# A transformer encoder in one kernel: every gate behind the next pair's second sum, four shared buffers for the weight sums, and the memory's squares in the first chunk

## The chip, the cores and the metric

The kernel runs on one core of a Trainium2 chip. The metric is the device time of one execution in microseconds; the time before is the median of three runs, 2031.19 us (2030.74 to 2033.74). TensorE (PE in the profile) does the matmuls, VectorE is DVE, ScalarE is ACT, GpSimd is POOL, SyncE is SP.

## What is computed

Two encoder layers on 512 tokens of width 1024. Each layer has a half-step feed-forward block, a mixer with several kinds of attention, an attention over 256 memory tokens, and a second half-step feed-forward block. The change lies in the feed-forward blocks, which compute, on normalised tokens:

```python
D_MODEL = 1024
SEQ = 512
DEPTH = 2
N_MEM = 256
D_FF = 2816

def swiglu(x, wg, wu, wd):
    return (jax.nn.silu(x @ wg) * (x @ wu)) @ wd
```

The memory tokens are normalised too (`rmsnorm`), once, and the sums of squares for that are computed inside the first feed-forward block.

## The kernel before

**Stages.** The program has seven stretches in the profile: feed-forward 1 of layer 0 (0 to 343 us), mixer and memory attention (to 718), feed-forward 2 (to 1038), feed-forward 1 of layer 1 (to 1367), its mixer and memory attention (to 1690), and the last feed-forward (to 2030). They are called the first to fourth stage below where only the four feed-forward blocks are meant.

**A split product.** Each float32 operand is split in two, a high part rounded to TensorE's format (`wh`, `sh`, `t1h`, `hh`; ScalarE, a copy) and the rest (`wl`, `sl`, `t1l`, `hl`; VectorE, a subtraction). A product is high times high, high times low and low times high. For weights `operand` (L529) does this, for each of the seven products of a pair; its results go in turn to two shared buffers `wh`/`wl` or, every third time, to the stage's own pair `sh`/`sl` (`f.n % 3 == 2`).

**Pairs.** The 22 blocks of the hidden width go in pairs. Pair 0 is a plain product (`plain_pair`). Pairs 1 to 10 each compute gate and up projections for 256 hidden columns with a Strassen-like scheme of seven products instead of eight. Each product is 24 matmuls of 128x256, in `product` (L565), a product every 2.72 us. By the name of their token operand they come in this order: `t1` (`sum_pair`: the weights' sum s1), `t2` (the same sum less w11, the "second sum", L607), `21` (`cross_pair`: w12), `t3` (the third sum s3), then the next pair's `11` (`open_pair`: w11), then `t4` (w22) and `22` (`close_pair`: w12 less the second sum). `t1` to `t4` are token combinations, split once per stage by `token_sums` (L480 to L485). The weight sum s1 and the third sum s3 are made by a fetch on SP (L550) and an accumulating DMA of a second quarter on POOL (L601 and L633); s3 is negated on ScalarE between them (L632). Buffers: three for s1, one for s3, three (`wf`) for plain weights.

**Results.** The products accumulate in PSUM and are collected in `gu` by copies on ScalarE (L588, L614, L627, L638, L651) and additions on VectorE (L639, L659). The *crossed copy* is L638, after `t3`. Then comes the *gate*: gs = gu times R (L688, R is the normalising factor per token), silu (L690), times up (L691); `hidden_done` makes sums and differences for the paired down-projection (L700) and splits the result (`hh` on ScalarE L450, `hl` on VectorE L454, `th`, `xh` likewise, L710 and L715). Before the change the gate of pairs 1, 2, 3 and 7 is written behind the low part of the next pair's second sum (`f.lowered`); all other gates are written at once.

**Down-projection.** The hidden width is taken in chunks of 6, 8 and 8 blocks. The first two are done by `paired_down` with the same seven-product scheme, after pairs 3 and 7; the last by `down` at the end, with an early block (`down_products`, L835) between the `t3` product and the last two products of pair 10, whose weights are split into `sh`/`sl` (`block` with `own`, L169).

**Heads.** While pair 0 still runs, the sum of squares of the tokens gives `factor` (L405), then four transposes (L418) and a copy (L419) give R. Pair 0's own gate is L422, L430 and L432. After pair 2's `cross_pair`, `set_aside` writes the eight token blocks (256 KB each) to DRAM (L802; in the first stage the input itself is used and nothing is written), to make room for the down-projection's sums.

**Memory's squares.** In the first stage `mem_stats` fetches four of the eight memory blocks at a time, squares them on ScalarE (L259) at pairs 3 and 4 and adds them on POOL (L260); at pair 6 it makes the factor.

**Order.** TensorE's order is the order in which the code is written. That of the other engines and of the DMA issues comes from a scheduler that simulates a timeline; `high_priority` and `behind` (issue after a given instruction) steer it. On each engine the instructions then run in that order, and a DMA queue works in order too.

## Time and profile before

| | |
|---|---|
| median of three runs | 2031.19 us (2030.74 to 2033.74) |
| profiled execution | 2032.02 us, span 2030.2 us, granted clock 0.998 |
| TensorE | 2008.5 us, 99% of the span |
| VectorE | 1597.6 us, 79% |
| ScalarE | 1278.1 us, 63% |
| POOL | 357.0 us, 18% |
| chain that ended last | TensorE 93% |

In a timeline a row has the start in us, the length, the engine, the line, the operation, the tiles written and read (without buffer numbers), their shapes, the count of merged instructions, and in brackets the idle time before them and what ended it. Rows of windows have, for each engine asked for, busy time and count, then the clock granted to TensorE (1 is full), the DMA engines' share and GB/s. Rows of DMAs have the tile, the issuing engine's queue, the count, the size of one and the us from issue to landing.

### The profile page before, as it was taken

To read this page: it belongs to the slowest core of one execution; us is meant where nothing else is said; L and a number is where in the kernel's file an instruction comes from. 1 tells how busy PE (TensorE), PEld (TensorE's weight loads), DVE (VectorE), ACT (ScalarE), POOL (GpSimd) and SP (SyncE) were. 2 spreads that over 40 slices of the span, in tenths; PEclk is the share of its full clock that TensorE was granted. 3 is DMA by queue.
4 is the path that set the end of the run, shared out by engine and by line. 5 is a ranking of instruction groups with operands and counts; after the bars stand their busy time and mean duration, and the time that the engine had idled before them with its cause. 6 is when DMAs were issued, how large, how long until landed. Compare 5 with 4: busy or idle time off the path is not lost.

```text
span 2030.2 us, 35251 instructions
## 1 busy us (share of the span) xinstructions
PE 2008.5 (99%) x13849; PEld 1843.1 (91%) x13853; DVE 1597.6 (79%) x2363; ACT 1278.1 (63%) x1955; POOL 357.0 (18%) x339
## 2 busy tenths in 40 slices
PE   9999999999999999999999999999999999999999
PEld 7999998888888899999989999988888888999997
DVE  8979776699676798888679797864668788979784
ACT  7667564656786576665657665745768566766572
POOL 1021001356531111100010101003353111010100
PEclk9999999999999999999999999999999999999999
DMA  7777755322241277776467777544224324777763
GB/s 233 199 200 190 192 164 167 99 79 84 95 139 61 65 235 187 209 189 183 144 177 206 207 187 188 176 140 140 94 84 125 104 73 141 221 209 193 183 177 98
DMA packets 102263, 316.53 MB, mean 156 GB/s; under 512 B 11472, under 2 KB 14672, under 8 KB 102096
## 3 DMA queue, kind: packets, MB, share of 16 engines
q1 hardware_dynamic: 85680, 257.12, 38.6%
q0 software_dynamic: 16128, 56.63, 16.1%
q8 instruction: 109, 1.79, 0.3%
q14 instruction: 58, 0.48, 0.1%
q10 hardware_dynamic: 288, 0.52, 0.1%
HBM read 301.64 MB, written 12.58 MB: 155 GB/s over the span
## 4 chain that ended last, share of the span: by engine, by line
PE 93%; DVE 2%; ACT 2%; DMA 2%; issue 1%; POOL 0%; SPq 0%; DVEq 0%; ACTq 0%; POOLq 0%
PE ps_pa L565 35%; PE ps_pb L565 13%; PE ps_pa L958 13%; PE ps_pa L904 5%; PE ps_pa L835 4%; PE ps_pb L835 4%; PE ps_pb L1071 3%; PE ps_pa L399 2%; PE ps_pa L1561 2%; PE ps_pa L1392 2%; PE ps_pb L1124 1%; PE ps_pb L904 1%; PE ps_pb L1097 1%; PE ps_pa L1291 1%; PE ps_pb L399 1%; DMA s<-l_ffn_wq 1%
## 5 line engine op out<-in xcount | busy, mean ns | idle before, releaser
L169 ACT ACTIVATE wh<-wf 128x1024 fp32r<-128x1024 f32 (+1 forms) x155 | 154.4, 1002 | 178.7 <-issue 37.8
L541 ACT ACTIVATE wh<-s 128x1024 fp32r<-128x1024 f32 (+1 forms) x164 | 168.8, 1029 | 134.6 <-PE ps_pa L565 30.0
L542 DVE TENSOR_TENSOR wl<-s,wh 128x1024 fp32r<-128x1024 f32 (+1 forms) x164 | 193.6, 1182 | 57.9 <-ACT wh L541 55.7
L171 DVE TENSOR_TENSOR wl<-wf,wh 128x1024 fp32r<-128x1024 f32 (+1 forms) x110 | 128.9, 1177 | 43.1 <-ACT wh L169 39.8
L541 ACT ACTIVATE wh<-wf 128x1024 fp32r<-128x1024 f32 (+1 forms) x100 | 103.3, 1033 | 65.4 <-PE ps_pa L565 46.3
L171 POOL TENSOR_TENSOR wl<-wf,wh 128x1024 fp32r<-128x1024 f32 (+1 forms) x45 | 100.0, 2221 | 205.3 <-ACT wh L169 143.1
L542 DVE TENSOR_TENSOR wl<-wf,wh 128x1024 fp32r<-128x1024 f32 (+1 forms) x100 | 118.3, 1186 | 9.9 <-ACT wh L541 9.8
L633 POOL DMA_DIRECT2D s<-l_ffn_wq x40 | 35.1, 879 | 510.3 <-ACT s L632 234.7
L958 PE MATMUL ps_pa<-wh,xh 128*128 128x512 f32 x384 | 121.7, 398 | 0.0
L958 PE MATMUL ps_pa<-wh,xl 128*128 128x512 f32 x384 | 118.8, 391 | 0.0
L958 PE MATMUL ps_pa<-wl,xh 128*128 128x512 f32 x384 | 118.7, 390 | 0.0
L542 DVE TENSOR_TENSOR sl<-wf,sh 128x1024 fp32r<-128x1024 f32 (+1 forms) x68 | 80.3, 1180 | 19.8 <-ACT sh L541 19.8
L541 ACT ACTIVATE sh<-wf 128x1024 fp32r<-128x1024 f32 (+1 forms) x68 | 69.3, 1020 | 34.8 <-PE ps_pa L565 19.3
L958 PEld LDWEIGHTS ps_pa<-wh,xl 128*128 128x128 f32 x384 | 72.1, 188 | 15.7
L958 PEld LDWEIGHTS ps_pa<-wl,xh 128*128 128x128 f32 x384 | 72.0, 188 | 15.6
L542 DVE TENSOR_TENSOR sl<-s,sh 128x1024 fp32r<-128x1024 f32 (+1 forms) x60 | 71.1, 1185 | 17.9 <-ACT sh L541 17.8
L541 ACT ACTIVATE sh<-s 128x1024 fp32r<-128x1024 f32 (+1 forms) x60 | 62.0, 1033 | 36.7 <-PE ps_pb L565 12.9
L1086 ACT ACTIVATE e<-e,m 128x128 f32<-128x128 f32 (+3 forms) x128 | 70.7, 554 | 21.7 <-DVE m L1085 21.5
L958 PEld LDWEIGHTS ps_pa<-wh,xh 128*128 128x128 f32 x384 | 69.2, 188 | 12.3
L601 POOL DMA_DIRECT2D s<-l_ffn_wq x40 | 37.0, 932 | 236.6 <-DMA s<-l_ffn_wq 106.5
L565 PE MATMUL ps_pa<-xh,wh 128*128 128x256 f32 x472 | 73.6, 277 | 0.0
L565 PE MATMUL ps_pa<-xl,wh 128*128 128x256 f32 x472 | 73.1, 276 | 0.0
(460 smaller groups left out, 6204.1 us busy)
## 6 DMA issues: line engine op xcount, KB each, us to landing
wf<-l_ffn_wq SPq DMA_DIRECT2D x120, 512.0 KB, 4.5
s<-l_ffn_wq SPq DMA_DIRECT2D x80, 512.0 KB, 4.4
s<-l_ffn_wq POOLq DMA_DIRECT2D x80, 512.0 KB, 7.9
wf<-l_w_in SPq DMA_DIRECT2D x48, 512.0 KB, 3.4
wf<-l_ffn_wd SPq DMA_DIRECT2D x32, 512.0 KB, 3.7
wf<-l_ffn_wdq SPq DMA_DIRECT2D x24, 512.0 KB, 4.8
wf<-l_ffn_wdq SPq DMA_DIRECT2D x24, 384.0 KB, 3.7
s<-l_ffn_wdq SPq DMA_DIRECT2D x16, 512.0 KB, 3.8
```

The costliest lines, as they stand in the source:

```text
L169: self.leading = nc.scalar.activation(wh[:, sl], w[:, sl], AF.Copy)
L171: eng.tensor_sub(wl[:, sl], w[:, sl], wh.bitcast(F32)[:, sl])
L399: nc.tensor.matmul(p, w[a][:, k * P:(k + 1) * P], xs[k][c], start=k == order[0] and a == c == 0, stop=k == order[-1] and a == 1)
L541: self.leading = nc.scalar.activation(h, t, AF.Copy)
L542: self.parted = nc.vector.tensor_sub(l, t, h.bitcast(F32))
L565: self.nc.tensor.matmul(bank[:, z * 256:z * 256 + 256], w[a][:, o:o + P], xs[k][b], start=first and n == 0, stop=n == len(ops) - 1, skip_g ...
L835: self.nc.tensor.matmul(bank, w[a][:, j * P:(j + 1) * P], h, start=j == a == e == 0 and c < len(CHUNKS) - 1, stop=j == nb - 1 and (a, e) = ...
L904: nc.tensor.matmul(banks[dd], w[g, k // 2][a][:, o:o + P], parts(k)[b], start=k == first and a == b == 0, stop=k == last and a == 1)
L958: nc.tensor.matmul(banks[j], xs[k][a][:, j * P:(j + 1) * P], w[b][:, kk * 512:kk * 512 + 512], start=k == a == b == 0, stop=k == KB - 1 an ...
L1071: nc.tensor.matmul(bank[:, o:o + n], a, b[:, :n], start=c == 0, stop=c == len(ops) - 1)
L1086: nc.scalar.activation(e, e, AF.Exp, bias=m[:, i:i + 1], scale=-1.0, accum_out=rs[:, i:i + 1])
L1392: nc.tensor.matmul(banks[c][i], a[:, i * P:(i + 1) * P], b[:, c * 512:(c + 1) * 512], start=(k == 0 and n == 0), stop=(k == KB - 1 and n = ...
```

## The change

Six edits, in the four feed-forward stages:

1. Every gate but the last pair's is written behind the low part of the next pair's second sum, and the rounding of its result (`hh`, and the rest of `hidden_parts` with it) behind the crossed copy of that next pair.
2. s1 and s3 share one set of four buffers instead of three and one, in `paired_down` too.
3. The early block of the last chunk is written as two runs: four blocks through all three kinds of product, then two.
4. The rotation of the operand buffers begins at 2, so the first operand of pair 1 (w11) gets the stage's own tiles, and all later ones move by two places.
5. The copies after `t2` and `t3` (L614 and L638 before) get high priority, and the low part of pair 1's s1 is put behind `factor`.
6. The memory blocks are fetched all at once at pair 2; the squares come in one run ahead of the first paired down-projection, their additions on VectorE instead of POOL.

What this does to the order: VectorE at the opening of pair 1 in the second stage, before. `s1` is the weight sum (L542 its high part's remainder, L607 the second sum), t2l to t4l the token combinations, gs pair 0's gate, `wf` w12.

```order
L542 TENSOR_TENSOR wl_8117<-s1_8113,wh_8116 128x1024
L405 COPY factor_8006<-r_8004 128x4
L607 TENSOR_TENSOR s1_8113<-s1_8113,wf_8055 128x1024
L483 TENSOR_TENSOR t2l_8151<-tq_8032,t2h_8149 128x1024
L419 COPY R_8088<-ps_pb_8087 128x512
L542 TENSOR_TENSOR sl_8156<-s1_8113,sh_8154 128x1024
L542 TENSOR_TENSOR wl_8188<-wf_8185,wh_8187 128x1024
L422 TENSOR_TENSOR gs_8094<-ps_pa_7907,R_8088 128x512
L422 TENSOR_TENSOR gs_8094<-ps_pa_7969,R_8088 128x512
L483 TENSOR_TENSOR t3l_8227<-tq_8033,t3h_8225 128x1024
```

The same place on VectorE after the change:

```order
L407 COPY factor_8005<-r_8003 128x4
L546 TENSOR_TENSOR wl_8119<-s1_8115,wh_8118 128x1024
L421 COPY R_8090<-ps_pb_8089 128x512
L611 TENSOR_TENSOR s1_8115<-s1_8115,wf_8054 128x1024
L486 TENSOR_TENSOR t2l_8153<-tq_8031,t2h_8151 128x1024
L424 TENSOR_TENSOR gs_8096<-ps_pa_7906,R_8090 128x512
L424 TENSOR_TENSOR gs_8096<-ps_pa_7968,R_8090 128x512
L486 TENSOR_TENSOR t3l_8226<-tq_8032,t3h_8224 128x1024
L546 TENSOR_TENSOR wl_8156<-s1_8115,wh_8155 128x1024
L546 TENSOR_TENSOR sl_8187<-wf_8184,sh_8186 128x1024
```

The second sum's low part (sl_8156 before, wl_8156 after) has moved behind pair 0's two multiplications by R and behind t3l, and the factor ahead of the first sum's low part. The first and the fourth stage show the same; in the third the second sum's low part stays ahead of these three.

SP's DMA issues in the same place, before: s1 and s3 are weight sums of pairs 1 to 3, wf_8055 is w11 and wf_8185 w12 of pair 1, wf_8256 w11 of pair 2, kept the set-aside writes.

```order
L550 DMA s1_8113<-l0_ffn2_wq 128x1024
L550 DMA wf_8055<-l0_ffn2_wq 128x1024
L550 DMA s3_8217<-l0_ffn2_wq 128x1024
L550 DMA s1_8355<-l0_ffn2_wq 128x1024
L550 DMA s1_8612<-l0_ffn2_wq 128x1024
L550 DMA wf_8185<-l0_ffn2_wq 128x1024
L550 DMA wf_8256<-l0_ffn2_wq 128x1024
L550 DMA wf_8289<-l0_ffn2_wq 128x1024
L550 DMA s3_8469<-l0_ffn2_wq 128x1024
L802 DMA kept_8503<-x_6744 128x512 x2
```

And after; wf_8184 is now w12 of pair 1:

```order
L554 DMA s1_8115<-l0_ffn2_wq 128x1024
L554 DMA wf_8054<-l0_ffn2_wq 128x1024
L554 DMA s3_8216<-l0_ffn2_wq 128x1024
L554 DMA s1_8354<-l0_ffn2_wq 128x1024
L554 DMA s3_8454<-l0_ffn2_wq 128x1024
L808 DMA kept_8502<-x_6743 128x512 x2
L808 DMA kept_8502<-x_6750 128x512 x2
L808 DMA kept_8502<-x_7138 128x512
L554 DMA wf_8184<-l0_ffn2_wq 128x1024
L808 DMA kept_8502<-x_7138 128x512
```

The third sum of pair 2 has moved up to the fifth place, and five of the eight writes, which are tied to it, stand ahead of w12. The fourth stage shows the same; in the third all eight stand ahead of w12.

VectorE at pair 5 of the second stage, before and then after: s1 is pair 5's sum, the first row its second sum (before L607, after L611), gs the gate of pair 4.

```order
L607 TENSOR_TENSOR s1_9471<-s1_9471,wf_9357 128x1024
L659 TENSOR_TENSOR gu_8788<-gu_8788,ps_pb_9210 128x2x256
L542 TENSOR_TENSOR wl_9535<-wf_9532,wh_9534 128x1024
L688 TENSOR_TENSOR gs_9451<-gu_8788,R_8088 128x1024
L542 TENSOR_TENSOR sl_9504<-s1_9471,sh_9503 128x1024
```

```order
L611 TENSOR_TENSOR s1_9451<-s1_9451,wf_9356 128x1024
L665 TENSOR_TENSOR gu_8787<-gu_8787,ps_pb_9209 128x2x256
L546 TENSOR_TENSOR sl_9520<-wf_9517,sh_9519 128x1024
L546 TENSOR_TENSOR wl_9484<-s1_9451,wh_9483 128x1024
L694 TENSOR_TENSOR gs_9512<-gu_8787,R_8090 128x1024
```

The gate's multiplication has gone from ahead of the second sum's low part to behind it.

The diff, without the lines that only pass an argument on:

```diff
-            f = self.f = SimpleNamespace(pre=pre, ctx=ctx, hp=pool("h"), tp=pool("t"), H={}, n=0, taken=None, own=False, low=None, gate=None, ahead=None, spread=None, macc=None,
+            f = self.f = SimpleNamespace(pre=pre, ctx=ctx, hp=pool("h"), tp=pool("t"), H={}, n=2, taken=None, own=False, low=None, gate=None, ahead=None, spread=None, macc=None,
...
+                hide = None
                 if f.gate is not None:
                     f.gate, gate = None, f.gate
-                    gate(f.lowered)
+                    hide = gate(f.lowered)
...
                 self.cross_pair(pair)
+                if hide is not None:
+                    hide()
...
-                    self.down_products(c, early, LEAD + REST, False)
+                    self.down_products(c, early, LEAD + REST, False, range(CHUNKS[c] - 4))
+                    self.down_products(c, early, LEAD + REST, False, range(CHUNKS[c] - 4, CHUNKS[c] - 2))
...
-                    gate = self.close_pair(old, False)
-                    if p <= 2 or p in ends:
-                        f.gate = gate
-                    else:
-                        gate()
+                    f.gate = self.close_pair(old, False)
                     if c in PAIRED and p == ends[c]:
+                        if self.mem_r is None and c == 0:
+                            self.mem_squares()
                         self.paired_down(c)
...
-        nc.scalar.activation(hh[:, sl], h, AF.Copy)
+        with self.behind(after):
+            nc.scalar.activation(hh[:, sl], h, AF.Copy)
...
-        self.parted = nc.vector.tensor_sub(l, t, h.bitcast(F32))
+        with self.behind(after):
+            self.parted = nc.vector.tensor_sub(l, t, h.bitcast(F32))
...
-            pair.s = f.tp.tile([P, 1024], F32, name="s1", tag="s1", bufs=3)
+            pair.s = f.tp.tile([P, 1024], F32, name="s1", tag="s1", bufs=4)
...
-            w = self.operand(pair.s)
+            w = self.operand(pair.s, None, f.factored if p == 1 else None)
...
-        nc.scalar.copy(self.corner(pair, 0, 1), self.halves(pair.y))
+        with self.tc.high_priority():
+            nc.scalar.copy(self.corner(pair, 0, 1), self.halves(pair.y))
...
-            s = f.tp.tile([P, 1024], F32, name="s3", tag="s3", bufs=1)
+            s = f.tp.tile([P, 1024], F32, name="s3", tag="s1", bufs=4)
...
-        f.taken = nc.scalar.copy(c, self.halves(pair.y))
+        with self.tc.high_priority():
+            f.taken = nc.scalar.copy(c, self.halves(pair.y))
...
-            self.hidden_done(p, gs, t)
+            return lambda: self.hidden_done(p, gs, t, False, f.taken)
...
+    def mem_squares(self):
+
+        with self.behind(self.leading):
+            for m in self.f.mem:
+                self.f.macc = self.square(self.f.macc, m, NMEM, self.nc.vector)
```

More of the change, by code (lines that the diff above doesn't have):

```diff
@@ L433, in hidden, with hidden_done @@
         self.hidden_done(p, gs, t, True)
-    def hidden_done(self, p, h, t, later=False):
+    def hidden_done(self, p, h, t, later=False, after=None):
         for c in PAIRED:
@@ L439, in hidden_done, with hidden_parts @@
             if 0 <= j < CHUNKS[c] // 2:
-                return self.hidden_sums(p, j, h, t, later)
-        self.hidden_parts(p, h, 0, later)
-    def hidden_parts(self, p, h, b0, later=False):
+                return self.hidden_sums(p, j, h, t, later, after)
+        self.hidden_parts(p, h, 0, later, after)
+    def hidden_parts(self, p, h, b0, later=False, after=None):
         nc, f = self.nc, self.f
@@ L527, in own_tiles, with operand @@
         return tiles
-    def operand(self, t, own=None):
+    def operand(self, t, own=None, after=None):
         nc, f = self.nc, self.f
@@ L691, in gates, with hidden_sums @@
             nc.vector.tensor_mul(two(gs), two(t), gu[:, :, 1, :])
-            self.hidden_done(p, gs, t)
+            return lambda: self.hidden_done(p, gs, t, False, f.taken)
         return gates
-    def hidden_sums(self, p, j, h, t, later):
+    def hidden_sums(self, p, j, h, t, later, after):
         nc, f = self.nc, self.f
@@ L704, in hidden_sums @@
         sub(part(t, 2), part(h, 2), part(t, 1))
-        self.hidden_parts(p, h, 0, later)
+        self.hidden_parts(p, h, 0, later, after)
         two = [f.hp.tile([P, S], F32R, name=n, tag="T", bufs=max(CHUNKS)) for n in ("th", "tl")]
@@ L1439, in mem_keys @@
         return kh, kl, vp
+    def mem_squares(self):
+        with self.behind(self.leading):
+            for m in self.f.mem:
+                self.f.macc = self.square(self.f.macc, m, NMEM, self.nc.vector)
     def mem_stats(self, p):
         nc, f = self.nc, self.f
-        if p in MEM_SQUARES:
-            with self.behind(self.leading):
-                for m in f.mem:
-                    f.macc = self.square(f.macc, m, NMEM)
-        if p + 1 in MEM_SQUARES:
-            n = KB // len(MEM_SQUARES)
-            f.mem, loaded = [], self.loaded
-            for k in range(MEM_SQUARES.index(p + 1) * n, MEM_SQUARES.index(p + 1) * n + n):
-                if k % 2 == 0:
-                    two = f.hp.tile([P, S], F32, name="mem", tag="T", bufs=max(CHUNKS))
-                m = two[:, k % 2 * NMEM:k % 2 * NMEM + NMEM]
+        if p == MEM_FETCH:
+            rooms = [f.hp.tile([P, 1024], F32, name="mem", tag="H", bufs=max(CHUNKS))]
+            rooms += [f.hp.tile([P, S], F32, name="mem", tag="T", bufs=max(CHUNKS)) for _ in range(2)]
+            f.mem = [t[:, o:o + NMEM] for t in rooms for o in range(0, t.shape[-1], NMEM)]
+            loaded = self.loaded
+            for k, m in enumerate(f.mem):
                 with self.behind(loaded):
                     nc.sync.dma_start(m, self.I["memT"][k * P:(k + 1) * P, :])
-                f.mem.append(m)
         if p == MEM_FACTOR:
```

6 lines of the change are left out of this document (3 added, 3 removed).

## The prediction

> **What bounds the kernel now.** I read the page first (busy times, chain), then TensorE's waits, then the timelines of the engines around each of these waits. From the page, the busy times and the chain of work that ended last, by engine:
>
> ```profile
> PE 2008.5 (99%) x13849; PEld 1843.1 (91%) x13853; DVE 1597.6 (79%) x2363; ACT 1278.1 (63%) x1955; POOL 357.0 (18%) x339
> PE 93%; DVE 2%; ACT 2%; DMA 2%; issue 1%; POOL 0%; SPq 0%; DVEq 0%; ACTq 0%; POOLq 0%
> ```
>
> TensorE is the bound, and the change gives it the same products. So the time moves only by what TensorE waits, and by the clock it is granted. The waits of TensorE in the four feed-forward stages (engine, bank and line, what it waited for: us in all, times, longest):
>
> ```profile
> PE ps_pa L565 <- DVE wl L542: 3.0, 5, 0.7
> PE ps_pa L835 <- ACT sh L169: 2.8, 4, 0.7
> PE ps_pa L565 <- DVE sl L542: 2.6, 4, 0.7
> PE ps_pa L565 <- ACT gu L614: 2.6, 1, 2.6
> PE ps_pa L565 <- ACT gu L638: 1.1, 1, 1.1
> PE ps_pa L565 <- ACT wh L541: 0.7, 1, 0.7
> PE ps_pb L418 <- DVE factor L405: 0.4, 1, 0.4
> ```
>
> These 13.2 us are all that the change can win directly; whatever it adds can be much more, since a late operand stops TensorE outright.
>
> **Pair 4 of the first stage.** Timelines of POOL, ACT and TensorE, two stretches of TensorE (busy time, matmul records, granted clock), and one of all engines in the paired down-projection before (PE, PEld, DVE, ACT, POOL busy):
>
> ```profile
> 120.45 1.18 POOL L633 DMA_DIRECT2D s<-l_ffn_wq  x1
> 129.66 1.06 ACT L541 ACTIVATE wh<-s 128x1024 fp32r<-128x1024 f32 x1 [5.73 <-DMA s<-l_ffn_wq]
> 133.14 0.74 PE L565 MATMUL ps_pa<-t3h,wh 128*128 128x256 f32 x4 [2.55 <-ACT gu L614]
> 134.00:138.00 4.00, 4.00 (x23) 0.58 0.50 172
> 138.00:142.00 4.00, 4.00 (x37) 1.00 0.57 187
> 92.00:106.00 14.00, 14.00 (x126) 14.00 (x125) 9.66 (x12) 8.57 (x12) 2.59 (x3) 1.00 0.73 192
> ```
>
> The third sum's accumulating DMA was issued at 120.45 and held ScalarE until 129.66; the copies behind it stopped TensorE for 2.55 us. Then the clock fell: 23 matmuls in 4 us where the next 4 us have 37, so 14 matmuls of 4/37 us, 1.5 us. The change lets the third sums take any of four buffers, so that the fetch and the DMA come a sum earlier, and takes the memory squares' additions off POOL. I count all of it as won, with the wait of about 0.5 us on wl (the first row of the waits) that the same pair has two products earlier: 0.5 + 2.55 + 1.5 = 4.6 us. The additions go to VectorE in the first paired down-projection, where it is busy for 9.66 of 14 us; that idle time hides them and I cost them at nothing. Without this cover they would be at most 7 times 0.64 us, half of what the two 128x512 multiplications of a later row take.
>
> **The gates.** Pair 5 of the second stage, on VectorE and TensorE:
>
> ```profile
> 843.80 1.22 DVE L688 TENSOR_TENSOR gs<-gu,R 128x1024 f32<-128x1024 f32 x1
> 844.94 1.22 DVE L542 TENSOR_TENSOR sl<-s,sh 128x1024 fp32r<-128x1024 f32 x1
> 846.21 0.75 PE L565 MATMUL ps_pa<-t2h,sl 128*128 128x256 f32 x4 [0.65 <-DVE sl L542]
> ```
>
> The gate's multiplication (L688) stands ahead of the second sum's low part, and TensorE waits 0.65 us for it. All nine waits on wl and sl are of this kind or that of pair 4. Every gate now stands behind that low part, so I take them as gone: 3.0 + 2.6 less the 0.5 counted above, 5.1 us. What is late next on VectorE is the gate itself, which nobody needs before the pair's third product.
>
> **The final pair.** The early block's weights waited for the kernel's own pair of operand tiles, which the third product was still reading:
>
> ```profile
> 987.85 1.06 ACT L169 ACTIVATE sh<-wf 128x1024 fp32r<-128x1024 f32 x1 [0.74 <-PE ps_pa L565]
> 988.96 1.67 PE L835 MATMUL ps_pa<-hh,sh 128*128 128x512 f32 x6 [0.69 <-ACT sh L169]
> 989.77 0.57 ACT L638 COPY gu<-ps_pa 128x512 f32<-128x512 f32 x1
> ```
>
> With the rotation begun at 2, the second product has these tiles, and they are free one and a half products earlier: four waits of 0.7 go. But pair 9's rounding now waits for the crossed copy: copy 0.57, hh 1.06, hl 1.2 and some 0.8 of handovers make about 3.6 us after the third product, and the split block reaches hl after 12 matmuls and 2 of the next six; six take 1.67 with the last one's run-out, so 14 take between 3.2 and 3.9. I give back 0.4 each: 2.8 - 1.6 = 1.2 us. Of the remaining 2.2 us (gu L638, wh, factor) I count 1.3, since factor now precedes a 1.2 us operation and the other two lie in stretches whose order is changed. Together the change wins 4.6 + 5.1 + 1.2 + 1.3 = 12.2 us; 14.5 if the last three groups go entirely, about 8 if half of the gate's waits reappear.
>
> **The heads: VectorE.** The other side is where each stage opens its first pair. Second stage, before:
>
> ```profile
> 736.19 0.65 PE L418 MATMUL ps_pb<-ident,factor 128*128 128x128 f32 x4 [0.35 <-DVE factor L405]
> 737.23 1.22 DVE L483 TENSOR_TENSOR t2l<-tq,t2h 128x1024 fp32r<-128x1024 f32 x1
> 738.97 1.21 DVE L542 TENSOR_TENSOR sl<-s,sh 128x1024 fp32r<-128x1024 f32 x1
> 740.35 0.62 PE L565 MATMUL ps_pa<-t2h,sl 128*128 128x256 f32 x4
> 741.24 1.28 DVE L422 TENSOR_TENSOR gs<-ps_pa,R 128x512 f32<-128x512 f32 x2
> 742.43 1.22 DVE L483 TENSOR_TENSOR t3l<-tq,t3h 128x1024 fp32r<-128x1024 f32 x1
> ```
>
> The second sum's low part was done at 740.18, 0.2 us before its use. In the changed order two multiplications by R (1.28) and t3l (1.14 at its cadence) come between t2l and it, and the copy of R, which needs the four transposes at 736.19, is moved ahead of the lowered sum. VectorE then goes through R from 736.7 to 737.3, lowered to 738.4, t2l to 739.6, the two to 740.8, t3l to 741.9, the low part to 743.1, and TensorE, which comes to it at 740.35, waits 2.7 us. The first, second and fourth stage have this order; the third keeps the low part ahead. Bounds: nothing if the operations overlap, 8.1 us in all.
>
> **The heads: SP.** Third sums now have room, so the third sum of pair 2 is fetched at once; the set-aside writes, which stood behind it, come with it, and five of them (eight in the third stage) go ahead of pair 1's w12. In the second stage: SP's queue; DMAs with the us to landing, an s issued at 720.06, w12 at 722.85, and two accumulations issued at 727.6 and 728.1; the second product:
>
> ```profile
> 722.85 14.86 SPq L550 DMA_DIRECT2D wf<-l_ffn_wq  x3
> s<-l_ffn_wq SPq DMA_DIRECT2D x1, 512.0 KB, 11.3
> wf<-l_ffn_wq SPq DMA_DIRECT2D x1, 512.0 KB, 12.4
> s<-l_ffn_wq POOLq DMA_DIRECT2D x2, 512.0 KB, 10.3
> 739.45 0.62 PE L565 MATMUL ps_pa<-t2h,sh 128*128 128x256 f32 x4
> ```
>
> So s landed at 731.4 and w12 at 735.2, 3.8 us for 512 KB beside the accumulations, of which the second landed by about 739. ScalarE splits w12 and then t4 before the second sum, in both kernels, so a late w12 makes the second product late. What a write costs, from three of the third stage, issued at 1074.9, 1075.6 and 1076.8, the last beside an accumulation:
>
> ```profile
> kept<-x SPq DMA_DIRECT2D x1, 256.0 KB, 6.7
> kept<-x SPq DMA_DIRECT2D x1, 256.0 KB, 6.4
> kept<-x SPq DMA_DIRECT2D x1, 256.0 KB, 8.4
> ```
>
> They landed at 1081.6, 1082.0 and 1085.2: some 0.5 us alone, 3.2 beside an accumulation; by bytes, half of w12's 3.8, it would be 1.9. Five at 0.6 put w12 at 738.2, five at 1.9 at 744.7. Two slow ones take the time until the accumulations end, three go fast: 735.2 + 2 x 2.5 + 3 x 0.6 = 742. ScalarE then needs w12 (0.95), t4 (0.95) and the second sum (1.05), and TensorE starts at 745.0 instead of 739.1 (739.45 without the factor's 0.35): 6.0 us, with bounds 2.7 (VectorE's order alone) and 8.7.
>
> The fourth stage (w12 issued at 1709.2, second product) and the third (w12 issued at 1050.0, and its product with xh, for which w12 is due):
>
> ```profile
> wf<-l_ffn_wq SPq DMA_DIRECT2D x1, 512.0 KB, 11.4
> 1725.42 0.62 PE L565 MATMUL ps_pa<-t2h,sh 128*128 128x256 f32 x4
> wf<-l_ffn_wq SPq DMA_DIRECT2D x1, 512.0 KB, 8.6
> 1069.18 0.62 PE L565 MATMUL ps_pa<-xh,wh 128*128 128x256 f32 x4
> ```
>
> In the fourth w12 landed at 1720.6; the same 6.8 us put it at 1727.4, and 3 us of ScalarE start TensorE at 1730.4 instead of 1725.4: 5.0 us; I take 4.5, since its accumulations end sooner behind w12, bounds 2.7 and 7. In the third w12 landed at 1058.6, and 2 x 2.5 + 6 x 0.6 more is 1067, just in time for 1068.2 (its order splits the second sum first): nothing, bound 5 us. The first stage writes nothing aside: 2.7.
>
> After pair 4's stall of 2.55 us the clock cost 1.5; I charge the two long stalls that much each, 3.0, and keep 1.5 for the first stage as a bound.
>
> The Trainium skill ("TensorE: Matmul & The Clock Gate", Part 1) says that the clock drops to half only after an idle window of about 3.4 us. The rows above show a drop after 2.55 us, so here the trace goes first; by the page the drops at the heads would mostly be absent and the sum 3 us less.
>
> **The sum.** Losses 2.7 + 6.0 + 4.5 + 3.0 = 16.2 us, gains 12.2: +4.0. The profiled execution took 2032.0 us (span 2030.2 and 1.8 around it), 0.8 above the median of 2031.2; its 2036.0 becomes 2035.2 on the median's scale, and I round up to 2035.5 for the restarts.
>
> **The rivals.**
> - Writes hide (faster). If five writes cost 0.6 each, w12 comes at 738.2 and only VectorE's order decides: 3 times 2.7 = 8.1 against 12.2, 2031.2 - 4.1 = 2027.1. It decides below about 740 for w12. For it: the two writes that landed 0.5 us apart. Against it: the one that took 3.2. Chance 0.20, half of it beyond 0.2%.
> - Heads cost nothing: both orders overlap with slack that I do not see; 2031.2 - 12.2 = 2019. The 0.2 us of slack at 740.18 speaks against it. Chance 0.09.
> - The clock stays full (the page's rule): 16.2 - 3.0 - 12.2 = +1.0, 2032.2. The window after pair 4 speaks against it. Chance 0.10.
> - The gates' waits move: VectorE is near its own bound in the pairs behind a head, and a later gate makes other low parts late; half of 12.2 goes, 16.2 - 6.1 = +10, 2041. For it: pair 2 of the first stage, busy 18.88 of 19 us (PE, PEld, DVE, ACT, POOL). Against it: pair 2's gate stood behind the second sum before. Chance 0.13.
>
> ```profile
> 54.00:73.00 19.00, 19.00 (x169) 19.00 (x168) 18.88 (x23) 14.65 (x19) 2.51 (x3) 1.00 0.76 216
> ```
>
> - The change does not do what it says: the orders show it does; only the sum may be nil, 2031. Chance 0.06.
>
> **How the numbers follow.** About 0.2% (4 us) is what a measurement of this kernel can tell from no change. The forecast itself has 0.42; its terms (w12 between 740 and 745, gains of 9 to 14) spread it from 2028 to 2043, so 0.31 of it is slower by over 0.2% and 0.11 within. Slower: 0.31 + 0.13 = 0.44; within: 0.11 + 0.10 + 0.10 + 0.06 = 0.37; faster: 0.10 + 0.09 = 0.19. The range 2023 to 2045 takes in all but the second rival and the far end of the fourth.
>
> **What would show it.** Right: in the second and fourth stage a stall of 4 to 6 us at the second product of pair 1, released by ScalarE's wh, with w12 landing after 740 and 1725, and a clock below 1 in the following 4 us; 2.7 us in the first stage released by VectorE's wl; no stall of 2.55 at pair 4 and no 0.7 waits at pairs 5 and 7. Wrong: w12 landing before 739, heads without stalls, or as many 0.7 us waits as before.

## The result: slower by one per cent, and the profile after

| | before | after |
|---|---|---|
| median of the runs, us | 2032.47 (2030.74 to 2035.36) | 2052.71 (2052.39 to 2058.19) |
| profiled execution, us (span) | 2032.02 (2030.2) | 2058.19 (2056.2) |
| ratio after / before, 95% interval | | 1.0105 (1.0083 to 1.0126) |

The changed kernel takes 20 us more, where 4 were forecast and 2045 was the end of the range. The profiled execution is the longest of its runs; its span is 26.0 us longer than that of before, and against this the rows below are summed. The page of after, the chain of work that ended last by engine:

```profile
PE 82%; DMA 7%; DVE 5%; ACT 3%; issue 2%; SPq 0%; POOL 0%; ACTq 0%; DVEq 0%; POOLq 0%
```

TensorE's share of the chain fell from 93% to 82%: DMAs, VectorE and ScalarE stand in it now. The rows of TensorE's waits that lie in the feed-forward stages say what released it (us in all, times, longest):

```profile
PE ps_pa L569 <- ACT gu L592: 15.6, 4, 6.5
PE ps_pa L569 <- ACT wh L544: 5.8, 3, 3.4
PE ps_pa L569 <- ACT ps_pa L761: 5.6, 8, 1.2
PE ps_pa L841 <- DVE hl L457: 1.8, 4, 0.5
...
PE ps_pa L569 <- ACT sh L544: 1.5, 1, 1.5
...
PE ps_pa L569 <- DVE wl L546: 0.9, 1, 0.9
PE ps_pb L569 <- DVE wl L546: 0.3, 1, 0.3
```

They come to 31.5 us, where the rows of before came to 13.2: 18 us more. (Both kernels also wait 1.3 us for xh in the plain product of pair 0; neither sum counts that.) The rest of the 26 is the clock. The granted clock of the core, before and then after:

```profile
core 0: 2030.2 us, clock 0.998
```

```profile
core 0: 2056.2 us, clock 0.994
```

0.6% of 2056 less 0.2% of 2030 is 8 us. What the change was to remove is gone: no wait on sl, none of 2.55 us at pair 4, and on wl only 0.9 us at the head of the first stage and 0.3 in its paired products. Two new groups took their place.

**The heads.** First row L592, four times, once in each stage. ScalarE at the head of the second stage, TensorE at its second product, and the queue of SP before it:

```profile
744.17 1.06 ACT L544 ACTIVATE sh<-wf 128x1024 fp32r<-128x1024 f32 x1 [7.50 <-DMA wf<-l_ffn_wq]
...
746.08 1.04 ACT L544 ACTIVATE wh<-s 128x1024 fp32r<-128x1024 f32 x1
747.02 0.56 ACT L592 COPY gu<-ps_pa 128x512 f32<-128x512 f32 x1
```

```profile
747.64 1.22 PE L569 MATMUL ps_pa<-t2h,wh 128*128 128x256 f32 x4 [6.28 <-ACT gu L592]
```

```profile
723.91 3.56 SPq L808 DMA_DIRECT2D kept<-x  x3
728.46 0.33 SPq L554 DMA_DIRECT2D wf<-l_ffn_wq  x1
```

And the clock behind it, in TensorE's windows (busy times of PE, PEld, DVE, ACT, POOL, granted clock, DMA share, GB/s):

```profile
745.41:748.82 3.41, 1.18 (x5) 1.18 (x6) 1.67 (x2) 3.39 (x5) 0.00 (x0) 0.50 0.56 229
748.82:752.23 3.41, 3.41 (x18) 3.41 (x17) 3.41 (x4) 2.08 (x2) 0.00 (x0) 0.50 0.07 22
```

This is the stall that the prediction described: the set-aside writes (kept) stand ahead of w12 (wf), which lands at 744.1; ScalarE has idled 7.5 us for it, then splits w12, t4 and the second sum, and only behind these comes the copy (L592) that gives the product its PSUM bank. The fourth stage has the same picture with 6.5 us, the first 1.66 for L592 and 0.9 for wl without any write, the third 1.10 (there w12 lands at 1078.8, and L592 again stands behind its split). In the first stage it is VectorE that makes the copy late, through ScalarE: the copy of R and the first sum's low part stand ahead of the lowered sum (L611), ScalarE idles for that, then splits two sums, and the copy L592 comes behind them at 38.88:

```profile
36.97 2.00 ACT L544 ACTIVATE wh<-s 128x1024 fp32r<-128x1024 f32 x2 [1.63 <-DVE s L611]
```

Behind the second stage's stall TensorE works 1.18 + 3.41 us at half the clock, behind the fourth's 5.4.

**The paired products, which the prediction did not speak of.** Their third sum is negated on ScalarE (L783; L777 before) before the accumulating DMA. What this operation made ScalarE wait, in all its 16 places, before and after:

```profile
  DMA s<-l_ffn_wdq: 14.7, 13
```

```profile
  DMA s<-l_ffn_wdq: 52.2, 16
```

The operation now runs earlier in ScalarE's order, before its own fetch has come: in pair 7 of the third stage it ran 6.3 us after the start of the second product in before, and it runs ahead of that product now. ScalarE and TensorE in pair 7 of the third stage, and TensorE's window behind (columns as above):

```profile
1227.10 1.06 ACT L783 ACTIVATE s<-s 128x1024 f32<-128x1024 f32 x1 [6.50 <-DMA s<-l_ffn_wdq]
...
1228.53 1.06 ACT L544 ACTIVATE wh<-s 128x1024 fp32r<-128x1024 f32 x1
```

```profile
1229.64 0.88 PE L569 MATMUL ps_pa<-t2h,wh 128*128 128x256 f32 x4 [3.44 <-ACT wh L544]
```

```profile
1230.10:1233.50 3.40, 3.40 (x18) 3.40 (x17) 3.40 (x4) 2.44 (x3) 0.00 (x0) 0.50 0.94 151
```

ScalarE idles 6.5 us on a negation that nobody needs yet; behind it stands the high part (wh) of the second sum, and TensorE waits 3.44 us for that, after which its clock is half for 3.4 us. The rows wh, ps_pa L761, sh and the 0.3 on wl of the waits above come to 13.2 us, and by the timelines ahead of each, 11.2 of them come behind this paired negation. Another 1.7 (at 825, 1156 and 1827 us) come behind the negation of the next plain pair's third sum (L637), for whose fetch ScalarE idles 1.6 to 2.8 us ahead of the paired operands, and 0.3 behind a late w12.

### The profile page after: what moved, and what is told of

Read it like the earlier page. It is cut to its first block, busy times and chain, and to the rows that moved or that the text cites. A ratio compares the mean times of both kernels' runs of the same rounds, so it can differ in the third digit from the quotient of the medians.

```text
span 2056.2 us, 35257 instructions
## 1 busy us (share of the span) xinstructions
PE 2016.2 (98%) x13853; PEld 1849.2 (90%) x13853; DVE 1596.7 (78%) x2370; ACT 1274.8 (62%) x1955; POOL 350.5 (17%) x332
## 4 chain that ended last, share of the span: by engine, by line
PE 82%; DMA 7%; DVE 5%; ACT 3%; issue 2%; SPq 0%; POOL 0%; ACTq 0%; DVEq 0%; POOLq 0%
PE ps_pa L569 30%; PE ps_pa L964 13%; PE ps_pb L569 11%; PE ps_pa L910 5%; PE ps_pb L841 4%; PE ps_pa L841 4%; PE ps_pb L1077 3%; DMA s<-l_ffn_wdq 2%; DMA wf<-l_ffn_wq 2%; PE ps_pa L1567 2%; PE ps_pa L1398 2%; DMA s<-l_ffn_wq 2%; PE ps_pb L1130 1%; DVE wl L546 1%; PE ps_pb L1103 1%
## 5 line engine op out<-in xcount | busy, mean ns | idle before, releaser
L169 ACT ACTIVATE wh<-wf 128x1024 fp32r<-128x1024 f32 (+1 forms) x155 | 154.4, 1003 | 176.4 <-issue 37.6
L544 ACT ACTIVATE wh<-s 128x1024 fp32r<-128x1024 f32 (+1 forms) x132 | 136.4, 1034 | 129.5 <-PE ps_pa L569 34.3
L546 DVE TENSOR_TENSOR wl<-s,wh 128x1024 fp32r<-128x1024 f32 (+1 forms) x132 | 156.9, 1189 | 64.9 <-ACT wh L544 64.0
L544 ACT ACTIVATE wh<-wf 128x1024 fp32r<-128x1024 f32 (+1 forms) x132 | 134.4, 1018 | 72.9 <-PE ps_pa L569 58.0
L546 DVE TENSOR_TENSOR wl<-wf,wh 128x1024 fp32r<-128x1024 f32 (+1 forms) x132 | 154.6, 1171 | 31.7 <-ACT wh L544 31.6
L171 DVE TENSOR_TENSOR wl<-wf,wh 128x1024 fp32r<-128x1024 f32 (+1 forms) x110 | 128.7, 1175 | 43.1 <-ACT wh L169 39.8
L605 POOL DMA_DIRECT2D s<-l_ffn_wq x40 | 35.7, 892 | 587.7 <-DMA s<-l_ffn_wq 349.9
L546 DVE TENSOR_TENSOR sl<-s,sh 128x1024 fp32r<-128x1024 f32 (+1 forms) x92 | 108.0, 1174 | 27.5 <-ACT sh L544 27.2
L544 ACT ACTIVATE sh<-s 128x1024 fp32r<-128x1024 f32 (+1 forms) x92 | 94.0, 1021 | 45.4 <-PE ps_pa L569 35.6
L569 PE MATMUL ps_pa<-xh,wl 128*128 128x256 f32 x560 | 86.9, 276 | 0.0
L964 PEld LDWEIGHTS ps_pa<-wl,xh 128*128 128x128 f32 x384 | 72.0, 188 | 15.6
L569 PEld LDWEIGHTS ps_pa<-xh,wl 128*128 128x128 f32 x560 | 74.2, 188 | 0.0
L569 PEld LDWEIGHTS ps_pa<-xh,wh 128*128 128x128 f32 x560 | 74.2, 188 | 0.0
```

What stands on the lines that cost most here:

```text
L169: self.leading = nc.scalar.activation(wh[:, sl], w[:, sl], AF.Copy)
L171: eng.tensor_sub(wl[:, sl], w[:, sl], wh.bitcast(F32)[:, sl])
L544: self.leading = nc.scalar.activation(h, t, AF.Copy)
L546: self.parted = nc.vector.tensor_sub(l, t, h.bitcast(F32))
L569: self.nc.tensor.matmul(bank[:, z * 256:z * 256 + 256], w[a][:, o:o + P], xs[k][b], start=first and n == 0, stop=n == len(ops) - 1, skip_g ...
L964: nc.tensor.matmul(banks[j], xs[k][a][:, j * P:(j + 1) * P], w[b][:, kk * 512:kk * 512 + 512], start=k == a == b == 0, stop=k == KB - 1 an ...
```

## The experiments

Theory S: the four shared buffers let third sums be fetched earlier, and everything tied to a fetch moves up with it: on SP's queue the set-aside writes ahead of w12, on ScalarE's the paired negation ahead of operands that TensorE is due to use. Rival H: VectorE's and ScalarE's order at the heads, which comes from the wait of pair 1's first low part for the factor, or from the rotation, costs most of it, and sharing is harmless. Rival G: the later gates move waits elsewhere. None of these kernels leaves out part of the computation. Times are medians, ratios are to before on the same chip with their 95% intervals.

### e1: the negation tied to w12's high part

```diff
                 self.fetch(v, p, 2)
-                nc.scalar.activation(v, v, AF.Copy, scale=-1.0)
+                with self.behind(self.leading):
+                    nc.scalar.activation(v, v, AF.Copy, scale=-1.0)
```

> The changed kernel, with one edit: in the paired down-projection the negation of the third sum is written behind the high part of w12, where it stood before. Theory A (the shared buffers let that negation move up ScalarE's queue, where it waits for its fetch ahead of the first sum's and second sum's high parts): the waits of 1 to 3.6 us at the second product of pair 7 and of the paired products go, 14 us of stalls and some 3 us of clock, so about 2052.7 - 15 = 2037 us, and the waits at the heads of the second and fourth stage stay at 6 us or more. Theory B (the later gates move VectorE's waits): no more than 4 us change, over 2048.

2096.89 us, 1.0308 (1.0290 to 1.0325): a miss, 44 us slower than after. The tie went too far. TensorE's waits:

```profile
PE ps_pa L569 <- ACT wh L544: 20.0, 8, 4.0
PE ps_pa L569 <- ACT sh L544: 16.7, 8, 5.1
```

Behind the negation stands the accumulating DMA. In the first stage, one of them, and the operand that waits for it (POOL, then ScalarE of e1):

```profile
212.66 0.86 POOL L785 DMA_DIRECT2D s<-l_ffn_wdq  x1 [11.11 <-ACT s L784]
```

```profile
220.30 1.06 ACT L544 ACTIVATE wh<-s 128x1024 fp32r<-128x1024 f32 x1 [3.64 <-DMA s<-l_ffn_wdq]
```

It is issued so late that ScalarE idles 3.64 us for its landing. So the negation has a window: too early it blocks ScalarE, too late it delays its own DMA.

### e2: the set-aside writes behind pair 2's w12

```diff
             pair.w12 = self.raw_quarter(p, 1)
+            f.crossing = self.loaded
...
-                with self.behind(self.loaded):
+                with self.behind(f.crossing):
                     nc.sync.dma_start(kept[d], self.x[d])
```

> The changed kernel, with one edit: the set-aside writes are written behind the fetch of pair 2's w12 instead of that of its third sum, so they go behind w12 of pair 1 and w11 of pair 2. Theory A (five writes ahead of w12 make the second product of pair 1 late): the stalls of 6.4 and 6.7 us in the second and fourth stage shrink to the 2.7 to 3 us of VectorE's order, and the half clock behind them goes, so about 2052.7 - 12 = 2041 us. Rival (VectorE's order at the head is what holds the product, and the writes ran beside it): less than 3 us change.

2043.90 us, 1.0058 (1.0043 to 1.0074): 8.8 us of the 20 come back, where 12 were expected. Its waits:

```profile
PE ps_pa L569 <- ACT ps_pa L762: 6.5, 7, 1.3
PE ps_pa L569 <- ACT gu L592: 5.0, 3, 1.7
PE ps_pa L569 <- ACT wh L544: 4.9, 5, 2.0
PE ps_pa L569 <- DVE wl L546: 2.7, 3, 0.9
```

The heads fall to 1.66 + 0.9 in each of three stages, which is what the first stage had without any write: the writes made the difference between 2.6 and 6.3, and the third stage's 1.1 is gone too. The negation's waits stay.

### e3: e1 and e2 together, and pair 0's gate behind the second sum's low part

```diff
...
+        with self.behind(f.lowered):
+            for b in range(2):
+                f.gated = nc.vector.tensor_mul(gs[:, b * S:(b + 1) * S], banks[b][0], f.R)
```

> The changed kernel with three edits: negation late, writes late, and pair 0's gate written behind the low part of pair 1's second sum. Theory A: all stalls that are new go, 2052.7 - 15 - 12 - 8 = about 2018 us, below the 2032 of the kernel before, whose waits of 0.7 and 2.55 us are gone too. Theory B: the waits reappear elsewhere, 2030 or more.

2080.14 us, 1.0239 (1.0224 to 1.0254), where 2018 was expected. It carries e1's damage (wh 17.0 and sh 14.8 us of waits) and says little; the wait of 0.9 on wl at the heads is gone, the 1.66 for L592 is not.

### e4: the third sums keep their own buffer

```diff
-            pair.s = f.tp.tile([P, 1024], F32, name="s1", tag="s1", bufs=4)
+            pair.s = f.tp.tile([P, 1024], F32, name="s1", tag="s1", bufs=3)
...
-            s = f.tp.tile([P, 1024], F32, name="s3", tag="s1", bufs=4)
+            s = f.tp.tile([P, 1024], F32, name="s3", tag="s3", bufs=1)
```

(and the same two lines in the paired products)

> The changed kernel with the buffers as before: three for first sums and one for third sums, all else changed. Theory A (sharing is what frees the writes and the negation): both new groups of stalls go, some 27 us, VectorE's 2.7 us at the heads stays, and the stall at pair 4 of the first stage may come back with up to 4.6: 2026 to 2031 us. Theory B (gates): within 5 us of the changed kernel's 2052.7.

2027.36 us, 0.9969 (0.9956 to 0.9981): with everything else of the change, the kernel is faster than before. Sharing costs 25 us here. Pair 4's stall does not come back. Left are the heads, and 1.8 us at the early block:

```profile
PE ps_pa L569 <- ACT gu L592: 5.0, 3, 1.7
PE ps_pa L569 <- DVE wl L546: 2.7, 3, 0.9
```

### e5: the negation tied less far

The first paired negation behind the crossed copy before it, the second behind the first product's high part.

```diff
+        gone = f.taken
...
-                nc.scalar.activation(v, v, AF.Copy, scale=-1.0)
+                with self.behind(gone):
+                    nc.scalar.activation(v, v, AF.Copy, scale=-1.0)
+                gone = self.leading
```

> The changed kernel, with one edit: the paired down-projection's first negation is written behind the crossed copy of the pair before it, as a pair's own negation is, and the second behind the high part of the first one's result. Late enough that its fetch has landed, and some 8 us earlier than in the first trial. Theory A (where the negation stands in ScalarE's queue decides): the stalls at the second product of pair 7 (1.3, 1.4 and 3.6 us) and at the paired second products (1 to 1.6 us) go without the new ones of the first trial, the heads keep theirs: 2052.7 - 14 = about 2038 us, between 2034 and 2042. Rival (any place of it costs as much): over 2048.

2043.57 us, 1.0052 (1.0037 to 1.0067): 9.1 us come back, less than the 14 expected. The waits on wh and sh are gone, the heads stay (the writes are where they were), and five waits remain in the paired products. Ahead of each of these five ScalarE has idled 2.5 to 4.4 us at L637, the negation of the next plain pair's third sum, for its fetch; this run tied only the paired one:

```profile
PE ps_pa L569 <- ACT gu L592: 15.9, 4, 6.6
PE ps_pa L569 <- ACT ps_pa L762: 5.8, 5, 1.5
```

### e6: sharing alone

The kernel before, with the four buffers alone:

```diff
-            pair.s = f.tp.tile([P, 1024], F32, name="s1", tag="s1", bufs=3)
+            pair.s = f.tp.tile([P, 1024], F32, name="s1", tag="s1", bufs=4)
...
-            s = f.tp.tile([P, 1024], F32, name="s3", tag="s3", bufs=1)
+            s = f.tp.tile([P, 1024], F32, name="s3", tag="s1", bufs=4)
```

> The kernel before, with one edit: first and third sums share four buffers. Theory A (sharing alone moves the writes ahead of w12 and the negation up): the second and fourth stage show 5 to 7 us at the second product of pair 1, and there are new stalls at paired second products; the old waits of 0.7 us stay: 2032 + 20 to 30 us, 2052 to 2062. Rival (only together with the later gates does it cost): within 5 us of 2032.

2065.40 us, 1.0158 (1.0143 to 1.0173): slower than the whole change, by more than was expected. So the rest of the change won back some 13 of the 33 us that sharing costs. Rival H falls as the main cause: there is no factor wait in this kernel, and its rotation begins at 0, and its heads stall 16.0 us in three places (6.7 at most).

### e7: own buffers, and the old rule for the gates

```diff
-                    f.gate = self.close_pair(old, False)
+                    gate = self.close_pair(old, False)
+                    if p <= 2 or p in ends:
+                        f.gate = gate
+                    else:
+                        gate()()
```

> The changed kernel with the buffers as before and the gates by the old rule (behind the next second sum for pairs 1, 2, 3 and 7 only). If the later gates are what takes away the eight waits of 0.7 us, these come back: 2027.4 + 5 = about 2032 us. If something else took them (the squares, the rotation), no change: 2026 to 2029.

2028.75 us, 0.9978 (0.9969 to 0.9988), against 0.9969 in e4: the gates are worth 0 to 2 us, which the intervals do not separate. Its waits show why:

```profile
PE ps_pa L573 <- DVE wl L550: 2.7, 3, 0.9
PE ps_pa L573 <- DVE sl L550: 2.5, 4, 0.7
```

Four waits on sl are there again, 2.5 us, but at pair 6 (the second stage's at 864 us), where before had four at pair 5 and four on wl at pair 7; the four of 1.8 on hl at the early block are away. None is left at pairs 5 and 7 (the 2.7 on wl lie at the heads), so the waits there went by another edit than the gate rule.

### e8: own buffers, R and pair 0's gate behind the second sum

```diff
-            nc.vector.tensor_copy(f.R, p)
...
+        with self.behind(f.lowered):
+            with self.tc.high_priority():
+                nc.vector.tensor_copy(f.R, p)
+            for b in range(2):
+                f.gated = nc.vector.tensor_mul(gs[:, b * S:(b + 1) * S], banks[b][0], f.R)
```

> The changed kernel with the buffers as before, and at each stage's opening the copy of R and pair 0's gate behind the low part of pair 1's second sum. If VectorE's order there costs 1.8 + 1.1 us in three stages, and half a clock window in one, as the timeline says: 2027.4 - 8.7 - 1.7 = about 2017 us, the fastest so far. If the wait is held by something else (ScalarE's order): less than 3 us gained, over 2024.

2033.06 us, 0.9996 (0.9986 to 1.0006), where 2017 was expected:

```profile
PE ps_pa L577 <- DVE gs L432: 7.6, 3, 2.6
```

The gate (now L432) frees the PSUM bank of the product behind the second: put later, it stops that one for 2.6 us in three stages. The stall was moved.

### e9 to e13: what orders the heads

e9 is e4 without the wait for the factor, with the early block's second run as hh, hh, hl:

```diff
-            w = self.operand(pair.s, None, f.factored if p == 1 else None)
+            w = self.operand(pair.s)
...
-                    self.down_products(c, early, LEAD + REST, False, range(CHUNKS[c] - 4, CHUNKS[c] - 2))
+                    self.down_products(c, early, LEAD[:1] + REST + LEAD[1:], False, range(CHUNKS[c] - 4, CHUNKS[c] - 2))
```

> The changed kernel with the buffers as before, with pair 1's first sum no longer put behind the factor, and with the early block's second run in the order hh, hh, hl. Theory (the one line that puts the low part behind the factor is what delays the second sum and lets the copy of R and pair 0's gate go ahead of it): the waits of 1.8 and 1.1 us at the heads go in three stages, with a half clock window, and the four 0.6 us waits at the early block shrink to 0.2: 2027.4 - 8.7 - 1.7 - 1.7 = about 2015 us. Rival (the heads wait for something else, as in the trial before): over 2024.

2030.47 us, 0.9983 (0.9974 to 0.9992), where 2015 was expected. The heads stall for another operand, the factor itself:

```profile
PE ps_pb L420 <- DVE factor L407: 8.9, 3, 3.9
```

VectorE of e9 at the head of the second stage:

```profile
730.52 1.22 DVE L546 TENSOR_TENSOR wl<-s,wh 128x1024 fp32r<-128x1024 f32 x1 [2.81 <-ACT wh L544]
...
734.45 1.22 DVE L611 TENSOR_TENSOR s<-s,wf 128x1024 f32<-128x1024 f32 x1
735.59 0.16 DVE L407 COPY factor<-r 128x4 f32<-128x4 f32 x1
```

The factor's copy, 0.16 us, stands behind token sums and the lowered sum, and TensorE transposes the factor before it goes on. The early block's waits are gone.

e10 is the shared kernel with e2's, e5's and e9's edits:

```diff
+                with self.behind(f.crossing):
...
+                with self.behind(gone):
...
+            w = self.operand(pair.s)
```

> The changed kernel with its four shared buffers, and all that they pushed forward held back: set-aside writes behind pair 2's w12, the paired negations behind the crossed copy and the first result, no wait for the factor, early block's second run reordered. If these orders are all that sharing costs, it ends where own buffers end, about 2015 to 2020 us. If sharing costs by itself (earlier fetches beside the others on the DMA engines): 2025 or more, with waits on fetches.

2030.31 us, 0.9991 (0.9982 to 1.0000): level with e9. Once the orders on SP and ScalarE are tied down, these two runs don't tell the shared buffers from own ones.

e11 is e9 with the memory squares as before (fetched for pairs 3 and 4, added on POOL):

```diff
-MEM_FETCH, MEM_FACTOR = 2, 6
+MEM_SQUARES, MEM_FACTOR = (3, 4), 6
...
-                        if self.mem_r is None and c == 0:
-                            self.mem_squares()
```

> The same as the first kernel of this call, but the memory's squares as before the change: in two halves at pairs 3 and 4, their additions on POOL. If the additions on POOL made the stall at pair 4 of the first stage, it comes back: 2.5 us of wait and 1.5 of clock, 4 to 5 us over the first kernel. If the gates cured it, no difference.

2037.25 us, 1.0025 (1.0015 to 1.0034), 6.8 more than e9: pair 4's stall is back, longer than before, and releases through the same copy as in before:

```profile
PE ps_pa L567 <- ACT gu L617: 4.9, 2, 4.5
```

e12 is e9 with the rotation of the operand tiles begun at 0, as before:

```diff
-            f = self.f = SimpleNamespace(pre=pre, ctx=ctx, hp=pool("h"), tp=pool("t"), H={}, n=2, taken=None, own=False, low=None, gate=None, ahead=None, spread=None, macc=None,
+            f = self.f = SimpleNamespace(pre=pre, ctx=ctx, hp=pool("h"), tp=pool("t"), H={}, n=0, taken=None, own=False, low=None, gate=None, ahead=None, spread=None, macc=None,
```

> The same as the first kernel of this call, but the operand rotation begins at 0 as before. If the rotation is what frees the early block's tiles, four waits of 0.7 us come back there: about 3 us over the first kernel. If not, no difference.

2024.12 us, 0.9959 (0.9946 to 0.9972): by its median the fastest of all, and faster than both kernels; the expectation had the sign wrong. With neither the factor wait nor the shift VectorE has at the heads the order of before, with the lowered sum ahead of R's copy, and TensorE goes through the second stage's head without a stop. VectorE and TensorE of e12 there:

```profile
731.32 0.16 DVE L407 COPY factor<-r 128x4 f32<-128x4 f32 x1
731.44 1.23 DVE L611 TENSOR_TENSOR s<-s,wf 128x1024 f32<-128x1024 f32 x1
...
734.32 1.22 DVE L546 TENSOR_TENSOR sl<-s,sh 128x1024 fp32r<-128x1024 f32 x1
```

```profile
734.42 0.62 PE L569 MATMUL ps_pb<-t1h,wl 128*128 128x256 f32 x4
734.87 0.62 PE L569 MATMUL ps_pa<-t2h,sh 128*128 128x256 f32 x4
```

What returns is the early block's wait on sh, 2.8 us in four. e13 is e12 with the factor wait put back, and the early block's run in the order of the change:

```diff
-            w = self.operand(pair.s)
+            w = self.operand(pair.s, None, f.factored if p == 1 else None)
```

> The kernel of e12 with the wait of the first low part for the factor kept (and the early block's second run in its own order). If that wait is what makes the heads stop, the heads of the first, second and fourth stage show about 1.8 + 1.05 us again, as in e4: 3 x 2.9 = 8.6 more than e12's 2024, so 2030 to 2034. If the rotation alone does it, the heads stay clean and the time is 2023 to 2026.

2033.39 us, 1.0006 (0.9997 to 1.0014), 9.3 more than e12. 2.5 us of that are waits on hl at the early block; the rest is the heads, which wait for L592 again (5.9 us in three) and bring three half-clock windows. The four kernels with own buffers, medians in us:

| | factor wait | no factor wait |
|---|---|---|
| rotation begun at 2 | 2027.4 (e4) | 2030.5 (e9) |
| rotation begun at 0 | 2033.4 (e13) | 2024.1 (e12) |

(e9 and e12 have the early block's second run reordered too, e4 and e13 not.) Each of the two edits costs time alone. Together they cost 3 us against neither by the medians, 2 by the ratios to before, and there the intervals of e4 and e12 overlap, so that this last difference is not shown.

### e14: the repaired shared kernel with rotation 0

e10 with e12's edit:

```diff
-            f = self.f = SimpleNamespace(pre=pre, ctx=ctx, hp=pool("h"), tp=pool("t"), H={}, n=2, taken=None, own=False, low=None, gate=None, ahead=None, spread=None, macc=None,
+            f = self.f = SimpleNamespace(pre=pre, ctx=ctx, hp=pool("h"), tp=pool("t"), H={}, n=0, taken=None, own=False, low=None, gate=None, ahead=None, spread=None, macc=None,
```

> The kernel of e10 (shared buffers, set-aside writes late, negations tied, no factor wait) with the rotation begun at 0 instead of 2. If rotation and factor wait together order the heads, the heads' 9 us and their two drops of the clock go and 4 x 0.86 us of the early block come back: 2030.3 - 6 = 2024 to 2026, as between e9 and e12. If the heads hang on the late transfers of the shared buffers, 2029 or more.

2028.31 us, 0.9980 (0.9971 to 0.9989): at the heads no wait for L592 or the factor is left (pair 1's third product still waits 1.6 us for L619 in the fourth stage), and the clock stays full, but it is 4.2 us behind e12. Most of what is left is the first mechanism once more. Its waits, and ScalarE in the second stage's paired products:

```profile
PE ps_pa L569 <- ACT ps_pa L763: 5.6, 5, 1.5
```

```profile
801.91 1.06 ACT L638 ACTIVATE s<-s 128x1024 f32<-128x1024 f32 x1 [3.86 <-DMA s<-l_ffn_wq]
```

As in e5 it is the next plain pair's negation (L638) that comes too soon and idles ScalarE for its fetch. e10 has the same wait, 4.7 us in four; that it is level with e9 doesn't make sharing free.

### e15: the squares alone, on the kernel before

The new function, its fetch and its call are put into the kernel before:

```diff
-MEM_SQUARES, MEM_FACTOR = (3, 4), 6
+MEM_FETCH, MEM_FACTOR = 2, 6
...
+                        if self.mem_r is None and c == 0:
+                            self.mem_squares()
```

> The kernel before with the memory squares alone moved (fetched after pair 2, multiplied and added on VectorE in the first paired down-projection). If they are what held pair 4 of the first stage, its waits of 0.5 and 2.55 us and the half-clock window go: 2032.5 - 4.6 = 2027 to 2029. If the single buffer of the third sums holds it, the stall stays and the time is 2032 to 2033.

2027.57 us, 0.9975 (0.9966 to 0.9985): 5.0 us won, as expected. Pair 4's stall and its half-clock window are gone while the third sums still have one buffer. Whether POOL's additions or the memory's loads beside the weights had held the accumulating DMA was not separated.

## Why the prediction was wrong, point by point

The sign was right, the size was not: +4.0 forecast, +20 by the medians, +26 in the profiled execution.

| step | forecast | after, by the rows above |
|---|---|---|
| pair 4 | -4.6 | -5.0 (e15) |
| gates' waits on sl and wl | -5.1 | gone from the rows |
| early block | -1.2 | 2.8 to 1.8: -1.0 |
| other waits | -1.3 | all three gone: -2.2 |
| head, first stage | +2.7 | 1.66 + 0.9: +2.6 |
| head, second stage | +6.0 | +6.3 |
| head, fourth stage | +4.5 | +6.5 |
| head, third stage | 0 | +1.1 |
| clock at the long stalls | +3.0 | half of 4.6 and 5.4: +5.0 |
| third sums' negations | not there | 13.2 in waits, 3.4 by the clock: +16.6 |

The last column comes to +25, of the 26 in the two spans.

- **The step that failed** is "Third sums now have room", which was followed on SP's queue at the heads and nowhere else. The same room lets the paired third sum be fetched earlier, and its negation, which is tied to nothing but its fetch, goes up ScalarE's order with it. The sum of the prediction has no term for this. With the clock behind these waits the last row of the table is 16.6 us, of which 1.7 come behind the next plain pair's negation and 0.3 behind a late w12; so the paired negation alone is about two thirds of the 22 us (26 less 4) by which the profiled execution missed the forecast. The trace of before held the hint: the negation already waited 14.7 us for its fetch. e4 and e6 show that sharing brings these waits, e5 that the paired negation's place is the cause of those on wh and sh; e1 shows that the place has limits on both sides.
- **Why pair 4 was cured** was put wrongly. The prediction named the four buffers first and the squares second; e4, e11 and e15 show the squares alone, and the credit to the buffers was what made sharing look useful.
- **The writes** were priced well. w12 was forecast at 742 on the scale of before; it landed at 744.1 in a trace that reaches this head 2.4 us later. Part of the agreement is luck: the prediction priced the writes by their landing alone, but w12 was also issued later (728.5 for 722.9, 3.2 us more than the trace's own delay) and then took 3.2 us longer to land. e2 confirms the chain. The rival in which they hide falls.
- **VectorE's order at the heads**: the size in the first stage is right (2.6 for 2.7), the path is not, so the agreement is luck in part. The prediction waited for the second sum's low part; of the wait, only 0.9 is that. Most of it is the copy L592 on ScalarE, which frees a PSUM bank and comes late because the lowered sum does. In these kernels it comes and goes with the factor wait (e13 against e12).
- **The clock**: the half speed after each long stall lasts longer than after pair 4: 4.6 and 5.4 us of work at half speed, 2.3 and 2.7 us lost, where I had charged pair 4's 1.5 each. Two of the paired stalls are followed by a window of 3.4 us at half the clock, 1.7 lost in each. The rival in which the clock stays full falls.
- **The gates**: all the waits that were to go went, but e7 puts their worth at 0 to 2 us: where the gates moved, the early block waits for hl instead, and with the old gates the waits at pairs 5 and 7 stay away and one at pair 6 comes instead, so another edit has moved them. The squares alone do not (e15 still waits four times each on sl and wl); which one does was not tried.
- **The third stage**: w12 came when forecast (1078.8 in a trace 12.7 us later here, so 1066 for 1067), in time for its own product; but in ScalarE's order the copy L592 stands behind its split, which the prediction overlooked, and TensorE waited 1.1 us for that. With the writes late (e2) this wait is gone.

## What to carry to other kernels

A buffer more doesn't only let a fetch start sooner: in engines that work in order, each instruction whose only tie is that fetch can move up as well in the scheduler's order, and may stop a queue in front of work that is due; follow every reader of the buffer, on every engine, and tie it to the work that it should come behind. A tie that is too late costs more than none (e1). An order at a bottleneck that is held by two edits together must be tested with both, one and neither, since single reversals can mislead: e9 and e13 each lost what e12 won.

## What the runs showed of the hardware

**When the clock falls.** The granted clock changes on a grid of 3.41 us, and what counts in these runs is how much of one such window TensorE idled. The heads of the first stage in e13 and e4 have the same two stalls (1.66 and 0.9 us). The windows of that grid, e13 and then e4 (PE, PEld, DVE, ACT, POOL busy, granted clock, DMA share, GB/s):

```profile
36.83:40.24 3.41, 1.45 (x10) 1.25 (x11) 3.41 (x5) 3.35 (x4) 0.00 (x0) 1.00 0.34 130
40.24:43.65 3.41, 3.41 (x18) 3.41 (x18) 3.41 (x4) 0.89 (x1) 0.00 (x0) 0.50 0.13 16
```

```profile
36.24:39.65 3.41, 2.29 (x21) 2.09 (x19) 3.41 (x5) 1.99 (x3) 0.00 (x0) 1.00 0.30 71
39.65:43.06 3.41, 1.99 (x14) 1.79 (x15) 3.41 (x4) 2.82 (x4) 0.00 (x0) 1.00 0.23 94
43.06:46.47 3.41, 3.41 (x32) 3.41 (x31) 3.41 (x5) 1.53 (x2) 0.00 (x0) 1.00 0.18 52
```

In e13 1.06 us of the first stall and all of the second fall into one window, which is busy for 1.45 of 3.41 us, and the next has half the clock: 18 rows of matmuls where a full one has 32. In e4 an edge lies between them, the windows are busy for 2.29 and 1.99, and the clock stays. Over all the profiles of this case, no window at full clock with under 1.5 us idle was followed by a half one, and each with over 1.95 us was, the first 10 us of a run left aside (there 1.3 us was enough in before and after). Between them both occur: 1.54 us in after was followed by a half one, 1.92 in e1 was not. The Trainium skill ("TensorE: Matmul & The Clock Gate", Part 1) gives such a window, about 3.4 us, and the runs agree with its length; it has the clock fall after an idle window, and here one that is idle for about half is enough. So the same stall costs 1.7 us more or not, by where it lies on the grid.

**Writes beside accumulating DMAs.** At the second stage's head of after, w12 took 15.6 us to land, against 12.4 in before, and the five writes about it (two ahead, three behind) a median of 15.3, against 6.4 to 8.4 for the three writes of before's third stage. Whether the accumulations or the writes' own number made them slow was not separated:

```profile
wf<-l_ffn_wq SPq DMA_DIRECT2D x1, 512.0 KB, 15.6
```

```profile
kept<-x SPq DMA_DIRECT2D x5, 256.0 KB, 15.3
```
